# A decoder layer on one core: weights and first operands in one lasting pool, the residual kept by tokens and turned in place, norms inside the gates, loads in program order

## The chip, the cores and the metric

One NeuronCore of a Trainium2 chip runs the whole kernel. Its engines work side by side, each through its own list of instructions in order: TensorE (PE: matmuls and transposes, results in PSUM, 8 banks of 128 x 512 float32), VectorE (DVE), ScalarE (ACT), GpSimd (POOL) and SyncE (SP), which here issues DMAs; POOL issues DMAs too. The metric is the time of one execution on the device in microseconds. An edit is judged by the medians of several runs, and its reasons by the profile of one execution.

## The reference, cut to what matters

```python
h = x                                            # (512 tokens, 1024)
h = h + 0.5 * swiglu(rms_norm(h, g_ffn1), w_ffn1_gu, w_ffn1_down)      # 1024 -> 2 x 2816 -> 1024
h = h + hybrid_mixer(rms_norm(h, g_mix), ...)    # gated conv + stick-breaking attention, 8 heads
h = h + memory_cross_attention(rms_norm(h, g_cross), rms_norm(mem, g_mem), ...)
h = h + 0.5 * swiglu(rms_norm(h, g_ffn2), w_ffn2_gu, w_ffn2_down)
out = rms_norm(h, g_final)

def swiglu(x, w_gu, w_down):
    gate, up = jnp.split(x @ w_gu, 2, axis=-1)
    return (jax.nn.silu(gate) * up) @ w_down
```

All is float32. The kernel multiplies in float32r: each operand is split into a high part `hi` and a low part `lo` (ScalarE makes `hi`, VectorE subtracts to make `lo`), and three matmuls, hi-hi, hi-lo and lo-hi, stand for one product.

## The kernel before, in words

**Four stages in a row:** FFN1, mixer, cross attention, FFN2. Each FFN is `up` (gate and up columns, then the gated values, spilled to DRAM) and `down`. Both use Strassen's scheme in Winograd's form: 7 products in place of 8 on halves of the operands. In `up` the columns come in blocks, five of 512 and one of 256 of each half; a block is 7 products in the order 1, 2, 5, 3, 6, 7, 4 (`UP`), each of two token tiles x 12 matmuls of 128x512, 24 in all. The left operands ("sides", `make_side`, L458) are made once, in the first block, from h times the norm's gain; their sums are on POOL (`sum_`, L465). The right operands are weight tiles of 512 KB: `x1`, `x2`, `x3` are loaded by SP (`load`, L392); sums of weights are made by a DMA on POOL that adds onto a loaded tile (L425) or by VectorE (L423). Each is split into `whi` and `wlo` (L117, L123) four units ahead of its use; loads are asked for five ahead. The first block uses three accumulating DMAs onto `x1` (`DMA_ONLY`).

**Norms.** The root mean square is not put into the operands: it scales rows of the products. `evac_of` multiplies by `r.cols` or its negative when a product leaves PSUM (L489, L492); so the first evacuation needs the norm. In FFN1 the squares are summed by 64 one-column matmuls (`norm1`, L662); in FFN2 by `rf.reduce` (L282) right after the mixer.

**Residual.** `h` is kept by channels: 8 chunks of 128 channels x 512 tokens. `down` makes tokens x channels, so it adds to a second copy `ht`, which FFN1 loads afresh (`in_xr`, 2 MB, POOL, L677) and FFN2 makes by 32 transposes (`turn_back`). After FFN1 32 transposes and 8 copies bring it back into `h` (L692, L693), and only then the mixer's operands `xm` are split (L119, L125).

**Mixer and cross attention** are a list of steps (`prog`), run by `run` (L164): weights come as 1 MB `raw` blocks by SP, halves are split two steps ahead, and each tile of results is 24 matmuls (`tile_step`). The mixer's pool holds 61 tiles of 128x512 for everything that lives.

**Memory and order.** SBUF is given out in phases: a phase's pools (`s` 14 sides, `w` weights, `e`, `a`, `h`; then the mixer's `w`, `a` 61, `c`) are given up at its end, and a tile of the next phase waits until the tiles that lay at its address are released. Tiles of one tag rotate through a fixed number of buffers. The program is written as one list, but a planner orders it: it goes through the instructions by priority, which is the order of writing, with estimated costs, and gives each engine the first instruction that is ready by its estimate. So work that is written later can be issued earlier, DMAs too.

Of the kernel before, what the change touches and what calls it, by code (L numbers as in the profile page):

```python
# [58 lines left out]
def layer_kernel(ctx, tc, xt, xr, memt, consts, g_final, w_gu1, w_dn1, w_dt1, w_qk, w_v, w_cx, w_cb, w_gate,  # L59
# [6 lines left out]
    dram = ctx.enter_context(tc.tile_pool(name="dram", bufs=1, space=bass.MemoryType.DRAM))  # L66
    pools = {}

# [14 lines left out]
    def act_tile(dt=F32, shape=(P, S)):  # L83
        return pools["a"].tile(list(shape), dt, tag="A", name=nm("a"))
# [26 lines left out]

    def mul(out_, a, b):
        nc.vector.tensor_tensor(out=out_, in0=a, in1=b, op=ALU.mult)  # L113
# [14 lines left out]
    def split(src, scale=None):  # L128

        hi = act_tile(F32R)  # L130
        lo = act_tile(F32R)
        split_hi(hi, src, scale)
        split_lo(lo, src, hi, scale)
        return hi, lo
# [29 lines left out]
    def run():  # L164
# [7 lines left out]
        def load():  # L172
            block = blocks[len(raws)]
            raw = pools["w"].tile([P, 2048], F32, tag="raw", name=nm("raw"), bufs=2)
            nc.sync.dma_start(out=raw[:, :block.shape[-1]], in_=block)
            raws.append(raw)

        def prepare(n):
# [4 lines left out]
            m = block.shape[-1] // 2  # L183
            hi = pools["w"].tile([P, 1024], F32R, tag="whi", name=nm("whi"))
            lo = pools["w"].tile([P, 1024], F32R, tag="wlo", name=nm("wlo"))
            src = raws[at][:, half * m:(half + 1) * m]
            split_hi(hi[:, :m], src)
            split_lo(lo[:, :m], src, hi[:, :m])
            parts[n] = tuple(t[:, :m].rearrange("p (k c) -> p k c", c=width) for t in (hi, lo))
# [67 lines left out]
    class Norm:  # L257


        def __init__(self, n=S):  # L260
            self.n, self.acc = n, None

        def square(self, h):
            sq = act_tile()[:, :self.n]
# [82 lines left out]
    class Plan:  # L347


        def __init__(self):  # L350
            self.steps, self.units, self.loads, self.loaded = [], [], [], 0

# [29 lines left out]
    class Weights:  # L382
# [4 lines left out]
        def __init__(self, plan, tiles, n, chain):  # L387

            self.plan, self.src, self.n, self.t, self.at, self.chain = plan, tiles, n, {}, {}, chain
            self.size = [q[0].shape[-1] for q in tiles]  # L390

        def load(self, x, u):  # L392
            def fn():
                tag = x if u < 4 or x == "x2" else x + "b"
                t = pools["w"].tile([P, 1024], F32, tag=tag, name=nm(x), bufs=xbufs[tag])[:, :self.size[u]]
                nc.sync.dma_start(out=t, in_=self.src[u][self.STARTS[x]])
                self.t[x, u] = t

            self.at[x, u] = self.plan.load(fn)
# [13 lines left out]
        def make(self, i, u):  # L413
            x, *then = self.chain[i]
            x = self.t[x, u]
            hi, lo = (pools["w"].tile([P, 1024], F32R, tag=tag, name=nm(tag), bufs=xbufs["w"])
                      for tag in ("whi", "wlo"))
# [6 lines left out]
            elif then[0] is not None:  # L424
                nc.gpsimd.dma_start(out=x, in_=self.src[u][then[0]], accum_op=ALU.add)  # L425
# [10 lines left out]
    xbufs = dict(x1=4, x1b=2, x2=3, x3=4, x3b=2, w=5)  # L436

    def up(g, r, w_gu, begin, norm):

        
        plan, parts = Plan(), {}
        spilled = dram.tile([P, 7, len(PAIRS), 256], F32, name=nm("spilled"))
        negr = spool.tile([P, 4], F32, tag="negr", name=nm("negr"))
# [6 lines left out]
        def prepare():  # L450
            x = [pools["e"].tile([P, 4, S], F32, tag="E", name=nm("x")) for _ in range(2)]
            box["a11"], box["a21"], box["a12"], box["a22"] = (x[k][:, :, s:s + 256] for k in range(2) for s in (0, 256))
            for k in range(KC):
                nc.scalar.activation(x[k // 4][:, k % 4, :], h[k], AF.Copy, scale=col(g, k))
# [780 lines left out]
```

## Time and profile before

| | us |
|---|---|
| median of 3 runs (1433.69 to 1441.03) | 1434.96 |
| the profiled execution | 1434.07 |
| its span, from the first to the last instruction | 1432.1 |
| TensorE busy in the span (97%) | 1384.2 |
| VectorE (66%), ScalarE (52%), POOL (8%) | 949.7, 737.9, 112.0 |
| moved by DMA | 211.37 MB, 148 GB/s on average |

In the profile TensorE's matmuls are pipelined: one starts before the last has ended, so its busy time is nearly the span whatever its pace. The pace is read from the starts of successive matmuls. FFN1's `up` runs from the start to about 252 us, its `down` to 366; the mixer and the cross attention to 1065; FFN2 to the end.

### The profile page before, as it was taken

How to read it: one execution, taken by the hardware profiler on the slowest of the kernel's cores; microseconds unless marked ns; L12 is line 12 of the kernel's file. 1: busy time of each engine (PE TensorE's matmuls, PEld its weight loads, DVE VectorE, ACT ScalarE, POOL GpSimd, SP SyncE). 2: the span in 40 equal slices, each digit the busy share in tenths (PEclk: the TensorE clock that was granted, in tenths of full speed). 3: DMA queues.
4: the chain of work that ended last, by engine and by line, in shares of the span. 5: the costliest groups of instructions: out<-in, count | busy, mean ns of one | idle time of the engine just before them, and what ended most of it. 6: DMA issues, size and time to landing. Idle time of an engine off the chain costs nothing.

```text
span 1432.1 us, 16800 instructions
## 1 busy us (share of the span) xinstructions
PE 1384.2 (97%) x6548; PEld 1160.5 (81%) x6548; DVE 949.7 (66%) x1264; ACT 737.9 (52%) x951; POOL 112.0 (8%) x118
## 2 busy tenths in 40 slices
PE   8999998899899999999999999999979999999997
PEld 7788888688788888888888888988866788878885
DVE  5777777597556663676544446745549787767796
ACT  6655555365455654555533225444436555555563
POOL 4011111110000000000000000000005111011010
PEclk8999999999999999999999999999998999999999
DMA  9877667962422133122232224353329666678571
GB/s 307 193 198 190 181 181 210 271 144 81 170 95 89 60 118 118 59 93 84 88 102 105 88 92 141 122 176 124 112 82 284 163 161 165 182 211 241 180 184 59
DMA packets 50031, 211.37 MB, mean 148 GB/s; under 512 B 5344, under 2 KB 5344, under 8 KB 41120
## 3 DMA queue, kind: packets, MB, share of 16 engines
q1 hardware_dynamic: 33200, 149.22, 30.1%
q0 software_dynamic: 16752, 61.09, 19.4%
q8 instruction: 51, 0.84, 0.2%
q14 instruction: 28, 0.23, 0.0%
HBM read 188.00 MB, written 22.28 MB: 147 GB/s over the span
## 4 chain that ended last, share of the span: by engine, by line
PE 79%; issue 7%; DMA 5%; DVE 5%; ACT 3%; POOL 1%; ACTq 0%; POOLq 0%; DVEq 0%
PE ps L153 13%; PE ps L155 13%; PE ps L154 13%; PE ps L433 10%; PE ps L434 10%; PE ps L432 10%; DMA x<-in_w_gu 3%; DVE wlo L123 2%; DMA x<-in_w_dn 2%; PE ps L250 2%; PE ps L249 2%; PE ps L251 2%; PE z L812 1%; ACT whi L117 1%; PE ps L523 1%
## 5 line engine op out<-in xcount | busy, mean ns | idle before, releaser
L432 PE MATMUL ps<-whi,s 128*128 128x512 f32 (+1 forms) x980 | 379.2, 388 | 17.0 <-ACT whi L117 9.5
L433 PE MATMUL ps<-wlo,s 128*128 128x512 f32 (+1 forms) x980 | 376.8, 385 | 6.4 <-DVE wlo L123 6.4
L434 PE MATMUL ps<-whi,s 128*128 128x512 f32 (+1 forms) x980 | 375.3, 383 | 0.1
L123 DVE TENSOR_TENSOR wlo<-x,whi 128x1024 fp32r<-128x1024 f32 (+1 forms) x238 | 291.6, 1232 | 114.3 <-ACT whi L117 113.1
L117 ACT ACTIVATE whi<-x 128x1024 fp32r<-128x1024 f32 (+1 forms) x238 | 243.8, 1032 | 208.7 <-PE ps L434 135.9
L153 PE MATMUL ps<-a,whi 128*128 128x512 f32 (+1 forms) x832 | 318.2, 383 | 3.8 <-ACT whi L117 3.8
L155 PE MATMUL ps<-a,wlo 128*128 128x512 f32 (+1 forms) x832 | 318.0, 382 | 0.0
L154 PE MATMUL ps<-a,whi 128*128 128x512 f32 (+1 forms) x832 | 317.7, 382 | 0.0
L117 ACT ACTIVATE whi<-raw 128x1024 fp32r<-128x1024 f32 x120 | 127.1, 1060 | 268.7 <-PE ps L154 176.0
L432 PEld LDWEIGHTS ps<-whi,s 128*128 128x128 f32 x980 | 188.7, 193 | 54.4 <-ACT whi L117 10.0
L433 PEld LDWEIGHTS ps<-wlo,s 128*128 128x128 f32 x980 | 188.7, 193 | 43.9 <-DVE wlo L123 10.2
L434 PEld LDWEIGHTS ps<-whi,s 128*128 128x128 f32 x980 | 188.6, 192 | 35.2 <-DVE s L123 0.8
L123 DVE TENSOR_TENSOR wlo<-raw,whi 128x1024 fp32r<-128x1024 f32 x120 | 146.7, 1223 | 84.2 <-ACT whi L117 84.0
L153 PEld LDWEIGHTS ps<-a,whi 128*128 128x128 f32 x832 | 157.1, 189 | 34.0 <-ACT whi L117 4.1
L155 PEld LDWEIGHTS ps<-a,wlo 128*128 128x128 f32 x832 | 157.0, 189 | 31.1 <-DVE wlo L123 0.8
L154 PEld LDWEIGHTS ps<-a,whi 128*128 128x128 f32 x832 | 157.0, 189 | 30.4 <-DVE a L125 0.2
L425 POOL DMA_DIRECT2D x<-in_w_gu x52 | 45.6, 876 | 1037.8 <-DVE wlo L123 1030.6
L423 DVE TENSOR_TENSOR x<-x,x 128x1024 f32<-128x1024 f32 (+1 forms) x60 | 71.0, 1188 | 1.2
L117 ACT ACTIVATE a<-a 128x512 fp32r<-128x512 f32 (+2 forms) x61 | 34.0, 557 | 59.4 <-DVE a L113 19.3
L113 DVE TENSOR_TENSOR a<-ps,a 128x512 f32<-128x512 f32 (+1 forms) x56 | 36.2, 651 | 38.9 <-PE ps L155 38.6
L123 DVE TENSOR_TENSOR a<-a,a 128x512 fp32r<-128x512 f32 (+2 forms) x61 | 36.3, 601 | 15.5 <-ACT a L117 11.6
L489 ACT ACTIVATE a<-ps,ny 128x512 f32<-128x512 f32 (+1 forms) x48 | 31.0, 650 | 29.4 <-PE ps L434 26.9
(163 smaller groups left out, 1312.1 us busy)
## 6 DMA issues: line engine op xcount, KB each, us to landing
x<-in_w_gu SPq DMA_DIRECT2D x66, 512.0 KB, 6.2
x<-in_w_gu POOLq DMA_DIRECT2D x52, 512.0 KB, 6.7
spilled<-e POOLq DMA_DIRECT2D x22, 896.0 KB, 7.6
x<-in_w_dn SPq DMA_DIRECT2D x30, 512.0 KB, 5.5
s<-spilled SPq DMA_DIRECT2D x28, 512.0 KB, 5.2
x<-in_w_dn POOLq DMA_DIRECT2D x20, 512.0 KB, 7.8
raw<-in_w_qk SPq DMA_DIRECT2D x8, 1024.0 KB, 4.9
raw<-in_w_v SPq DMA_DIRECT2D x8, 1024.0 KB, 4.9
```

The lines of the kernel that those rows point to most:

```text
L113: nc.vector.tensor_tensor(out=out_, in0=a, in1=b, op=ALU.mult)
L117: nc.scalar.activation(hi, src, AF.Copy)
L123: nc.vector.tensor_tensor(out=lo, in0=src, in1=hi.bitcast(F32), op=ALU.subtract)
L153: nc.tensor.matmul(ps, wh, xh, start=first, stop=False, **kw)
L154: nc.tensor.matmul(ps, wh, xl, start=False, stop=False, **kw)
L155: nc.tensor.matmul(ps, wl, xh, start=False, stop=last, **kw)
L423: nc.vector.tensor_tensor(out=dst, in0=dst, in1=src, op=ALU.add)
L425: nc.gpsimd.dma_start(out=x, in_=self.src[u][then[0]], accum_op=ALU.add)
L432: nc.tensor.matmul(ps, ah, bh, start=first and k == 0, stop=False, **kw)
L433: nc.tensor.matmul(ps, ah, bl, start=False, stop=False, **kw)
L434: nc.tensor.matmul(ps, al, bh, start=False, stop=last and k == len(parts) - 1, **kw)
L489: nc.scalar.activation(a[key], ps, func, scale=scale)
```

## The change

- **A lasting pool** `kept` is opened once and never given up: 4 weight tiles `x1`, 3 each of `whi` and `wlo`, 2 operand tiles `E`, 8 tiles `A`, 2 tiles `first`. FFN weights, the mixer's weights (now in halves of 512 KB) and the memory's operands come through the same `x1`, `whi`, `wlo`. The phases keep the rest: 12 side tiles (were 14), more weight tiles, and in the mixer 43 tiles (were 61); the 16 tiles of `xm`, and later of `xc`, lie in `A` and `E` (`front`), two pairs in `first`.
- **Tags turn between stages** (`tags`): `down` takes `x1` in the buffers of `x3` and the reverse; the second column block exchanges `x1` and `x2`.
- **Residual by tokens in place:** `h_all` becomes 128 x 8 x 4 x 128 and holds either channels or tokens. `in_xr` is stored in that order and loaded into it at the opening; `ht` is gone. After FFN1 the upper four chunks are turned between products 2 and 4 of `down`, the lower four in steps around the first half accumulations of head 0's q and k (`first_part`, upper chunks first). `turn_back` goes in place, chunk by chunk.
- **Norms in the gates:** products leave PSUM unscaled; `r.cols` scales Silu and the gate product. `norm1` is eight ScalarE squares with an accumulator over `h_all`; in both FFNs it is written behind side 5 in place of side 2.
- **Sides straight from h** with the gain in the split, by chunks; of the four sums one stays on POOL and three are on VectorE.
- **Loads in program order:** `dma` ties each DMA of a queue behind the previous one of that queue. In the first column block loads 4 to 7 go by POOL, and loads are asked for two ahead there. x comes in four quarters, weights between them.

```diff
+    kept = ctx.enter_context(tc.tile_pool(name="kept", bufs=1))
+    KEPT = dict(x1=((P, 1024), 4), whi=((P, 1024), 3), wlo=((P, 1024), 3), E=((P, 4, S), 2), A=((P, S), 8),
+                first=((P, 1024), 2))
+    def dma(out_, in_, queue="sync", **kw):
+        engine = getattr(nc, queue)
+        if queue in last:
+            with tc.issue_after(last[queue].ins):
+                last[queue] = engine.dma_start(out=out_, in_=in_, **kw)
+        else:
+            last[queue] = engine.dma_start(out=out_, in_=in_, **kw)
...
-                        self.start_loads(x.need + 1 + LOADS_AHEAD)
+                        self.start_loads(x.need + 1 + (LOADS_AHEAD if x.need not in (0, 1, 2, 3) else 2))
...
-                tag = x if u < 4 or x == "x2" else x + "b"
-                t = pools["w"].tile([P, 1024], F32, tag=tag, name=nm(x), bufs=xbufs[tag])[:, :self.size[u]]
-                nc.sync.dma_start(out=t, in_=self.src[u][self.STARTS[x]])
+                t = weight_tile(self.tags[x] + ("b" if u >= 4 and x != "x2" else ""))[:, :self.size[u]]
+                dma(t, self.src[u][self.STARTS[x]], "gpsimd" if place in self.plan.behind else "sync")
...
-                nc.gpsimd.dma_start(out=x, in_=self.src[u][then[0]], accum_op=ALU.add)
+                dma(x, self.src[u][then[0]], "gpsimd", accum_op=ALU.add)
...
+        def sums():
+            a11, a21, a12, a22 = (box[k] for k in ("a11", "a21", "a12", "a22"))
+            t, v, w = (half(side_tile(F32)) for _ in range(3))
+            for k in range(4):
+                nc.scalar.activation(t[:, k], a21[:, k], AF.Copy, scale=col(g, k))
+            nc.gpsimd.tensor_tensor(out=box["s3"], in0=a11, in1=a21, op=ALU.subtract)
+            for out_, x, g0, y, op in ((v, a22, 4, t, ALU.subtract), (w, a11, 0, v, ALU.add),
+                                       (box["s4"], a12, 4, w, ALU.subtract)):
+                for k in range(4):
+                    nc.vector.scalar_tensor_tensor(out=out_[:, k], in0=x[:, k], scalar=col(g, g0 + k), in1=y[:, k],
+                                                   op0=ALU.mult, op1=op)
...
+                for k in range(4):
+                    gain = col(g, gains + k)
+                    split_hi(half(hi)[:, k], src[:, k], gain)
+                    split_lo(half(lo)[:, k], src[:, k], half(hi)[:, k], gain)
+            if i == 5:
+                norm()
...
+        dma(cst, consts, "gpsimd")
+        quarter(0, 0)
+        plan.start_loads(2)
+        quarter(1, 0)
+        plan.start_loads(4)
+        quarter(0, 256)
+        quarter(1, 256)
...
+        dma(h_all, xr, "gpsimd")
+        sums = spool.tile([P, 8], F32, tag="sums1", name="sums0", bufs=2)
+        for tok in range(4):
+            for half in range(2):
+                squares_of(tok, half, sums)
+        r1.newton(add_halves(sums))
...
+        down(spilled, residual, w_dn1, w_dt1, lambda: None, squares,
+             {(2, 8): upper, (4, 4): lambda: turn_tokens(range(4), (0, 1))})
...
-    mixer_pools = phase(w=3, a=61, c=1)
+    mixer_pools = phase(a=43, c=1)
...
-    q_step(0)
-    k_step(0)
+    step(lambda: turn_tokens(range(4), (2,)))
+    step(lambda hi, lo: first_part(0, range(4, KC), hi, lo), qk_blocks[0], 0)
+    step(lower)
+    step(lambda hi, lo: first_part(1, range(4, KC), hi, lo), qk_blocks[0], 1)
+    step(lambda: first_part(0, range(4)))
+    step(lambda: first_part(1, range(4)))
```

## Rows read from the trace of the kernel before

**Rows 1.** the page's 40 slices of the span, TensorE's busy tenths

```profile
PE   8999998899899999999999999999979999999997
```

**Rows 2.** windows: PE, PEld, DVE, ACT, POOL busy (count), granted clock, DMA share, GB/s

```profile
0.00:64.30 64.30, 56.27 (x248) 46.35 (x249) 38.60 (x47) 42.09 (x53) 20.09 (x21) 0.89 0.95 276
10.00:20.00 10.00, 9.75 (x46) 7.84 (x46) 5.25 (x4) 9.47 (x14) 7.19 (x4) 0.78 1.05 366
...
278.60:290.90 12.30, 7.09 (x18) 5.04 (x18) 6.52 (x8) 7.01 (x8) 0.00 (x0) 0.72 0.57 185
366.30:379.70 13.40, 9.52 (x46) 7.38 (x45) 10.22 (x24) 12.51 (x23) 1.42 (x4) 0.75 0.55 190
1065.30:1122.40 57.10, 45.51 (x177) 34.92 (x177) 47.07 (x49) 36.82 (x44) 19.96 (x14) 0.88 0.96 273
```

**Rows 3.** timeline, PE at the opening: start, us, what, idle before, releaser

```profile
10.67 1.22 PE L432 MATMUL ps<-whi,s 128*128 128x512 f32 x2
...
63.63 0.39 PE L432 MATMUL ps<-whi,s 128*128 128x512 f32 x1
...
64.31 0.39 PE L432 MATMUL ps<-whi,s 128*128 128x512 f32 x1
```

**Rows 4.** groups by line and shape: count | busy us, mean ns | idle

```profile
L123 DVE TENSOR_TENSOR wlo<-raw,whi 128x1024 fp32r<-128x1024 f32 x120 | 146.7, 1223 | 84.2 <-ACT whi L117 84.0
...
L668 PE MATMUL z<-ones,a 128*128 128x1 f32 x64 | 9.1, 265 | 1.7 <-ACT a L666 1.7
...
L117 ACT ACTIVATE a<-a 128x256 fp32r<-128x256 f32 x16 | 6.6, 410 | 16.4 <-DVE a L789 14.0 <-DVE a L113 2.4
...
L125 DVE SCALAR_TENSOR_TENSOR a<-raw,cst,a 128x256 fp32r<-128x256 f32 x8 | 3.8, 480 | 0.0
```

**Rows 5.** timeline of the turn inside FFN1, POOL and ScalarE

```profile
263.78 0.79 POOL L677 DMA_DIRECT2D ht<-in_xr  x1 [4.75 <-DMA spilled<-e]
...
266.99 0.91 POOL L425 DMA_DIRECT2D x<-in_w_dn  x1 [2.42 <-DVE wlo L123]
...
282.37 1.06 ACT L117 ACTIVATE whi<-x 128x1024 fp32r<-128x1024 f32 x1 [10.63 <-DMA x<-in_w_dn]
```

**Rows 6.** timeline of PE, the same place in FFN2

```profile
1348.97 0.50 PE L433 MATMUL ps<-wlo,s 128*128 128x512 f32 x1 [0.81 <-DVE wlo L123]
```

**Rows 7.** timeline from FFN1 to the mixer: SP, PE, ACT

```profile
366.32 0.33 SPq L175 DMA_DIRECT2D raw<-in_w_qk  x1
...
366.36 3.79 PE L692 MATMUL ps<-ident,ht 128*128 128x128 f32 x32
373.99 0.79 PE L153 MATMUL ps<-a,whi 128*128 128x512 f32 x1 [3.84 <-ACT whi L117]
...
368.40 3.99 ACT L693 ACTIVATE h<-ps 128x512 f32<-128x512 f32 x8
```

**Rows 8.** timeline from the mixer to FFN2: SP, PE, DVE, POOL

```profile
1065.27 19.11 SPq L396 DMA_DIRECT2D x<-in_w_gu  x13
...
1073.71 1.22 PE L432 MATMUL ps<-whi,s 128*128 128x512 f32 x2 [5.01 <-ACT whi L117]
...
1092.66 0.57 PE L433 MATMUL ps<-wlo,s 128*128 128x512 f32 x1 [2.68 <-DVE wlo L123]
...
1077.10 10.27 DVE L123 TENSOR_TENSOR wlo<-x,whi 128x1024 fp32r<-128x1024 f32 x3
...
1079.67 3.27 POOL L465 TENSOR_TENSOR x<-x 128x1024 f32<-128x1024 f32 x1
```

**Rows 9.** timeline of SP, FFN1's down weights in the opening

```profile
26.82 0.46 SPq L396 DMA_DIRECT2D x<-in_w_dn  x1
```

**Rows 10.** DMA issues: queue, count, KB each, median us to landing

```profile
x<-in_w_gu POOLq DMA_DIRECT2D x52, 512.0 KB, 6.7
...
ht<-in_xr POOLq DMA_DIRECT2D x1, 2048.0 KB, 14.8
out_t<-ht SPq DMA_DIRECT2D x8, 256.0 KB, 2.2
```

More of the change, by code (lines that the diff above doesn't have):

```diff
@@ L182, in prepare @@
                 load()
[L183 to L189, printed above, removed]
+            hi, lo = kept_tile("whi", F32R), kept_tile("wlo", F32R)
+            src = raws[at][half]
+            split_hi(hi, src)
+            split_lo(lo, src, hi)
+            parts[n] = tuple(t.rearrange("p (k c) -> p k c", c=width) for t in (hi, lo))
         ready = used = 0
@@ L351, in __init__ @@
             self.steps, self.units, self.loads, self.loaded = [], [], [], 0
+            self.behind = ()
         def step(self, fn):
@@ L415, in make @@
             x = self.t[x, u]
-            hi, lo = (pools["w"].tile([P, 1024], F32R, tag=tag, name=nm(tag), bufs=xbufs["w"])
-                      for tag in ("whi", "wlo"))
+            parity["n"] += 1
+            hi, lo = (weight_tile(tag + ("" if parity["n"] % 5 < 3 else "b"), F32R) for tag in ("whi", "wlo"))
             m = self.size[u]
@@ new lines, in squares_of, with add_halves @@
+    def squares_of(tok, half, sums):
+        sq = side_tile(F32)[:, :S]
+        nc.scalar.activation(sq.rearrange("p (k c) -> p k c", c=P), residual(tok, half), AF.Square,
+                             accum_out=sums[:, 4 * half + tok:4 * half + tok + 1])
+    def add_halves(sums, n=4):
+        both = spool.tile([P, n], F32, tag="both", name=nm("both"))
+        nc.vector.tensor_tensor(out=both, in0=sums[:, :n], in1=sums[:, 4:4 + n], op=ALU.add)
+        return both
+    def norm1():
+        dma(h_all, xr, "gpsimd")
+        sums = spool.tile([P, 8], F32, tag="sums1", name="sums0", bufs=2)
+        for tok in range(4):
+            for half in range(2):
+                squares_of(tok, half, sums)
+        r1.newton(add_halves(sums))
@@ new lines, in layer_kernel, with turn_tokens, split_turned, squares @@
+    turned = {}
+    def turn_tokens(ms, ts):
+        for m in ms:
+            if m not in turned:
+                turned[m] = bank()
+        for t in ts:
+            for m in ms:
+                nc.tensor.transpose(out=turned[m][:, t * P:(t + 1) * P], in_=h_all[:, m, t, :], identity=ident)
+    def split_turned(ms):
+        for m in ms:
+            ps = turned.pop(m)
+            xm[m] = split(ps, col(G_MIX, m), room[(m + 4) % KC])
+            nc.scalar.activation(h[m], ps, AF.Copy)
+    with phase(s=12, w=1):
+        spilled = up(G_FFN1, r1, w_gu1, load_x, None, norm1)
+        sums = spool.tile([P, 8], F32, tag="sums1", name="sums1", bufs=2)
+        def squares(i, t):
+            part = {2: (t, 0), 3: (t, 1), 7: (t + 2, 1), 4: (t + 2, 0)}.get(i)
+            if part is not None:
+                squares_of(*part, sums)
+        def upper():
+            room.extend(front())
+            for m in range(4, KC):
+                turn_tokens([m], range(4))
+                split_turned([m])
+        down(spilled, residual, w_dn1, w_dt1, lambda: None, squares,
+             {(2, 8): upper, (4, 4): lambda: turn_tokens(range(4), (0, 1))})
+        rm.newton(add_halves(sums))
```

327 lines of the change are left out of this document (158 added, 169 removed).

## The prediction, made before the change was run

> **What bounds the kernel now.** I read the page's slices first [rows 1]: TensorE is full (a 9) in most slices, and the slices below that stand together, at the opening, at slices 7 and 8, at slice 11, at slice 30 and at the end. So TensorE bounds the kernel, and only the stretches in which it is interrupted can give time back. A busy TensorE is not one at its peak, so I then went by matmul starts: three steps take 0.68 us at the end of the first gate/up column block [rows 3], 0.227 us for a 128x512 matmul. A column block of gate/up is 7 products of 24 matmuls, 168, which is 38.1 us of work.
>
> The windows view [rows 2] then gives the losses. *Opening:* the first column block is done at 64.31 [rows 3] and holds 38.1 us of work; 26.2 us are lost. *Turn inside FFN1:* 278.6 to 290.9 holds 18 matmuls, 4.1 us of work in 12.3; 8.2 lost. *FFN1 to mixer:* 366.3 to 379.7 holds 32 transposes (3.8 us, [rows 7]) and 14 matmuls (3.2); 6.4 lost, of which 3.84 is idle [rows 7] and 2.6 the low clock after it. *Mixer to FFN2:* 1065.3 to 1122.4 is again one column block; 57.1 less 38.1 is 19.0 lost. In all 59.8 us. The granted clock's mean is 0.72 to 0.89 in these windows, so the lower level has a part in each.
>
> What each waits for is in the timeline. In the turn, the 2 MB load of `ht` goes out on POOL at 263.78, the accumulating weight load behind it at 266.99, and ScalarE's next `whi` starts at 282.37 after 10.63 us of idling [rows 5]. From FFN1 to the mixer, the transposes start at 366.36, eight copies occupy ScalarE from 368.40 for 3.99 us, and TensorE goes on at 373.99, released by a `whi` of a weight whose load was issued at 366.32 [rows 7]. From mixer to FFN2, 13 weight loads start together at 1065.27, when the mixer's pool is given up; TensorE goes on at 1073.71; then three `wlo` splits take 10.27 us of VectorE while POOL adds operands, and TensorE waits another 2.68 at 1092.66 [rows 8].
>
> **Opening.** The 64 one-column norm matmuls leave TensorE (9.1 us busy, [rows 4]); they become eight Square activations over a token-major copy of x. Side 1 becomes four gain splits of 128x256: 4 x 0.41 on ScalarE and 4 x 0.48 on VectorE [rows 4], where a whole scaled copy of x stood before. I put the first matmul at about 8.5 instead of 10.67 [rows 3]. The counterweight is bytes: `xr`, 2 MB, is now loaded here as well, on POOL, and `ht` no longer is later. I count what the first block's last product must have: 4 transfers of 512 KB for x, 4 for xr, 6 direct and 8 accumulating weight loads, and the first 5 of the next block, which are queued in between; 27 x 0.524 is 14.2 MB. At the 276 GB/s of the opening [rows 2] that is 51.3 us; the last split (1.06 and 1.22, [rows 4, 5]) and half a product (2.7) end the block at 56.3. Before, four loads of down weights (1.6 MB; the first is [rows 9]) were pulled ahead into the opening; in program order they are not. Gain 64.3 - 56.3 = 8.0. Bounds: with no byte waited for, 8.5 + 38.1 + 2.6 at the low clock = 49.2, a gain of 15.1; if the 2 MB stand wholly ahead of the next accumulation (7.6 us at 276 GB/s) and only the 2.2 us of the earlier start are won, -5.
>
> The norm's root is no longer a factor of the first evacuations but of Silu and of the gate product, so nothing of it holds a PSUM bank before the seventh product; its cover is five products of 5.4 us. The evacuations change operation, not length; I cost them at nothing.
>
> **Turn inside FFN1.** With the 2 MB gone, the accumulation has POOL's queue to itself. The same place in FFN2, which has no such load, idles only 0.81 before the matmul at 1348.97 [rows 6]. I take the difference of 7.4, and a little less for two side tiles fewer (12 for 14): 7.0 of 8.2. Bounds 4 and 8.2. The side loads are now one product later, with some 15 us before they are used.
>
> **FFN1 to mixer.** The upper half's 16 transposes, splits and copies go between the last two products of down, where TensorE has their banks and the evacuations are over; the lower half's run beside half accumulations of head 0 (2 x 12 matmuls, 5.4 us). After the last down matmul come an evacuation, four transposes (0.5, an eighth of [rows 7]), ScalarE's half of a split (0.5, as one of the eight copies) and VectorE's; VectorE needs 0.48 for half the size [rows 4], so under 1 each: at most 3 us, below that cover. The transposes themselves stay (3.8). The first mixer weights go into buffers that the finished `x3` chain frees, so their load no longer starts at the end. Gain 6 of 6.4; bounds 3 and 6.4. If the cover fails, the price is that 3 and the low clock again.
>
> **Mixer to FFN2.** The first four weight loads use the lasting `x1` buffers, and the first side the lasting `first` pair, with operands (the lower half of the residual) that are final four tiles of 24 matmuls, 22 us, before the mixer ends. Nothing of product 1 then waits for the mixer's pool, and the planner does pull ready work forward [rows 9]. I take it that product 1 follows the last mixer matmul at 1065.3. What is late next is product 5's weight, third in line: its accumulation is queued on POOL behind a load that may need the freed pool; three issues of 0.9 [rows 5], 6.7 to land [rows 10] and 2.3 to split give 1077.2, against 1076.2 for TensorE after two products. VectorE gets three of POOL's four sums as twelve 128x256 operations (12 x 0.48 = 5.8 us, [rows 4]), but is spared the 6.6 us by which three `wlo` went over 3 x 1.22 [rows 4, 8]. I leave 5 us of the 19.0 in place and take 14. Bounds: 18 if only one wait is left; 7 if only the shorter operand chain counts: an evacuation (1), four splits and one `whi` (4 x 0.41 + 1.06) after 1065.3 start product 1 at 1069.0, 4.7 earlier, and the 2.68 of waiting on POOL's sums goes.
>
> **Mixer and tail.** The mixer's pool keeps 43 tiles and 18 more in the lasting pool for the same 61; its weights come in halves of 512 KB at a low DMA share. No row shows what a shortage would cost, since TensorE has none there now. The output goes out in pieces of 512 B: nearest row 2.2 us for 256 KB [rows 10]. I charge 1.5 for both; bounds 0 and 6.
>
> **Sum.** 8.0 + 7.0 + 6.0 + 14.0 - 1.5 = 33.5. The profiled execution took 1434.07 (span 1432.1 and 2.0 around), 0.9 below the median of the runs; 1434.1 - 33.5 = **1400.6**.
>
> **A rule weighed.** POOL's row says 14.8 us for the 2 MB of xr while other loads ran [rows 10]. The Trainium skill, "DMA: Bandwidth & Descriptors", section "Anatomy of one DMA — SWDGE (gpsimd) path", gives a fixed 2.0 us and 436 GB/s beyond it for a DMA from that queue, an estimate of 6.8 us. The trace does not agree under load. By that rule the opening would not be byte-bound: the rival just below.
>
> **Rivals.** *The opening is not bound by bytes.* From 10 to 20 us the DMA engines moved 366 GB/s [rows 2]; at that rate 14.2 MB need 38.8 us and TensorE's own 49.2 decides. Total 1434.1 - (15.1 + 7 + 6 + 14 - 1.5) = 1393.5. For it: loads in need order. Against: 276 over the whole opening, with accumulations in it. Chance 0.12.
>
> *FFN2's start is not pulled forward*, so that the change there doesn't do what it is built for: the x3 loads, first on POOL, wait for the pool, everything behind them too, and splits stay behind the last residual add. Gain 7 instead of 14: 1407.6. For it: in one program order an early wait holds all later ones. Chance 0.17.
>
> *The opening loses*: xr stands ahead of the accumulations, and eight squares on ScalarE wait for it with every `whi` behind them. -5 instead of 8: 1413.6. For it: 14.8 us for the same load [rows 10]. Chance 0.14.
>
> *Slower: the pinned SP queue.* Loads can no longer pass one that waits for a buffer. If at each column block's start the third pair sits behind a second pair whose buffer is late, each of the eight boundaries between full blocks could wait half a landing (3.4, [rows 10]) and run 2.6 at the low clock, an estimate of 48 us: 1448.6. It decides from 33.5 / 8 = 4.2 us a boundary. Against: in full stretches loads already go out in that order, a few us ahead of their use. Chance 0.06. *The mixer runs short of tiles*: two gate evacuations wait and hold banks; if splits pile up behind them I price it at 20 us, 1420.6. Chance 0.06.
>
> **How the numbers follow.** The forecast has 0.45. All largest gains together (15.1 + 8.2 + 6.4 + 18) end at 1386, the smallest (-5 + 4 + 3 + 7 - 6) at 1431; together they are unlikely, and 1386 to 1424 leaves out the slow rival, the worst of the tile shortage and little else. About 0.5%, 7 us, is what a measurement of this kernel can tell from no change. Faster by more: all of the first four cases but a twentieth, and half of the tile shortage, 0.87. Within: 0.06. Slower: 0.07.
>
> **What would show it.** Right: no 128x1 matmul in the opening and the first block over before 58; no wait of several us near the last down accumulation of FFN1; mixer matmuls within 1 us of the last down matmul; product 1 of FFN2 directly behind the mixer, with its loads some 10 us earlier. Wrong: ScalarE idle on xr in the opening, SP's loads late at block boundaries, TensorE idle inside the mixer.

## The result, and the profile after it

The changed kernel took 1417.3 us (median; 1414.97 to 1421.65) where the kernel before, run beside it, took 1436.45: a ratio of 0.9867, 95% interval 0.9831 to 0.9903. The same code run again beside other kernels took 1412.9 (1411.77 to 1414.44), ratio 0.9829 (0.9811 to 0.9848). So the change gains 19 to 25 us where 33.5 were forecast; the time lies in the forecast range, 12 to 17 us above its point. The two medians of one code stand 4.4 us apart: totals nearer than that tell nothing here, and what follows goes by stretches of the profiles, between the starts of two matmuls. A block's end is the start of the matmul behind its 168th; the changed kernel already runs five of the next block among these. The kernel before has one profile, so that its own scatter is not in the gains below. One run of e3 (1716.9, granted clock 0.75 where the others had 0.98 to 0.99) is left out below.

| stretch (us) | before | after | after, again | gain | forecast |
|---|---|---|---|---|---|
| start to end of FFN1's block 0 | 64.31 | 61.56 | 61.87 | 2.4 to 2.8 | 8.0 |
| from there to the end of FFN1 | 301.82 | 301.32 | 300.92 | 0.5 to 0.9, with 24 transposes more (2.8): 3.3 to 3.7 | 7.0 |
| to the last matmul of the mixer | 698.95 | 689.32 | 689.36 | 9.6, of which those 2.8: 6.8 | 6.0 |
| to the end of FFN2's block 0 | 57.32 | 48.45 | 47.09 | 8.9 to 10.2 | 14.0 |
| to the last matmul of FFN2, and the tail | 309.71 | 312.62 | 310.82 | -2.9 to -1.1 | -1.5 |

(The 2.8 is 24/32 of the 3.79 in [rows 7].) Three terms of five came out at 0.3 to 0.7 of their size. The page and its windows, in the columns of [rows 1, 2]:

```profile
PE   7999998899999999999999999999999999999997
```

```profile
0.00:61.56 61.56, 48.82 (x184) 38.08 (x185) 43.85 (x70) 40.59 (x69) 15.74 (x24) 0.94 0.90 270
...
274.00:290.00 16.00, 13.27 (x52) 10.23 (x51) 12.78 (x15) 9.98 (x12) 0.00 (x0) 0.89 0.83 285
363.00:377.00 14.00, 14.00 (x68) 11.56 (x67) 10.63 (x32) 7.44 (x12) 0.00 (x0) 1.00 0.39 133
1052.20:1100.65 48.45, 43.59 (x179) 34.56 (x177) 38.22 (x65) 31.21 (x46) 7.94 (x10) 0.93 0.73 185
```

The dips of slices 11 and 30 are gone, and the mixer's start is full at full clock (363 to 377: busy 14.00 of 14.00, clock 1.00). The opening's slices and the turn still lose. The timeline of the opening, all engines, shows where:

```profile
8.84 1.22 PE L458 MATMUL ps<-whi,first 128*128 128x512 f32 x2 [4.00 <-ACT whi L144]
...
18.51 5.40 DVE L504 SCALAR_TENSOR_TENSOR s<-E,cst,s 128x256 f32<-128x256 f32 x8 [0.85 <-DMA E<-in_xt]
23.84 1.66 DVE L504 SCALAR_TENSOR_TENSOR E<-E,cst,s 128x256 f32<-128x256 f32 x4
...
12.57 0.91 POOL L135 DMA_DIRECT2D h<-in_xr  x1
19.42 2.63 POOL L500 TENSOR_TENSOR E<-E 128x1024 f32<-128x1024 f32 x1 [5.93 <-DVE s L504]
28.32 0.91 POOL L135 DMA_DIRECT2D x<-in_w_gu  x1 [6.26 <-DVE wlo L150]
...
27.83 0.80 PE L459 MATMUL ps<-wlo,s 128*128 128x512 f32 x1 [2.83 <-DVE wlo L150]
...
30.87 0.64 ACT L714 ACTIVATE s<-h 128x512 f32<-128x512 f32 x1 [4.76 <-DMA h<-in_xr]
...
36.74 0.57 ACT L534 ACTIVATE A<-ps 128x512 f32<-128x512 f32 x1
...
37.36 0.58 PE L458 MATMUL ps<-whi,s 128*128 128x512 f32 x1 [2.87 <-ACT A L534]
```

Product 1 starts at 8.84, as forecast (8.5). Then two queues are late. VectorE's operand sums wait for x's last quarter (18.51) and take 5.40 for eight beside POOL's one; product 5's `wlo` comes behind them, and the first accumulation behind a product 5 weight goes out only at 28.32. And ScalarE idles 4.76 until `xr` has landed, 18.3 us after its issue at 12.57; the eight squares follow, then a split of product 3's side, and behind that, at 36.74, the copy that frees product 3's bank. The low clock stood from 27.4 to 30.8 and again from 37.6 to 41.1, each time from about the end of one of these stalls of TensorE. After 37.36 TensorE waits for nothing more in this opening.

The turn, in the same view:

```profile
243.18 0.47 SPq L135 DMA_DIRECT2D x3b<-in_w_dn  x1
243.69 0.52 SPq L135 DMA_DIRECT2D x3b<-in_w_dt  x1
...
267.10 0.90 POOL L135 DMA_DIRECT2D x3b<-in_w_dn  x1 [9.11 <-DVE wlo L150]
...
276.06 1.06 ACT L144 ACTIVATE whib<-x3b 128x1024 fp32r<-128x1024 f32 x1 [5.27 <-DMA x3b<-in_w_dn]
...
279.34 0.50 PE L458 MATMUL ps<-whib,s 128*128 128x512 f32 x1 [2.24 <-ACT s L144]
```

ScalarE's wait on an accumulation has shrunk from 10.63 [rows 5] to 5.27, but TensorE's next wait, 2.24, is on a side load. Those loads need the last write of `spilled`. The view of DMA issues, cut to 255 to 258 us, has that write in the changed kernel (queue, count, size, us to landing), and cut to 255 to 259 us the same write in the kernel before:

```profile
spilled<-E POOLq DMA_DIRECT2D x1, 896.0 KB, 9.0
```

```profile
spilled<-e POOLq DMA_DIRECT2D x1, 896.0 KB, 5.1
```

And from the mixer to FFN2:

```profile
1022.16 37.23 SPq L135 DMA_DIRECT2D x<-in_w_gu  x8
...
1055.42 1.87 PE L308 MATMUL z<-ones,A 128*128 128x1 f32 x8 [2.83 <-DVE A L299]
1057.15 0.77 PE L458 MATMUL ps<-whi,first 128*128 128x512 f32 x1
```

The weights load from 1022 on, 30 us before the mixer's last matmul; in [rows 8] they start with its end. But product 1 starts 4.95 us behind the mixer's last matmul (1052.20): the norm's eight one-column matmuls stand ahead of it in TensorE's order and wait for VectorE's sum of squares.

### The profile page after: what moved, and what is told of

It is laid out like the page before. It is cut to its first block, busy times and chain, and to the rows that moved or that the text cites. A ratio compares the mean times of both kernels' runs of the same rounds, so it can differ in the third digit from the quotient of the medians.

```text
span 1413.3 us, 16964 instructions
## 1 busy us (share of the span) xinstructions
PE 1369.7 (97%) x6484; PEld 1147.5 (81%) x6484; DVE 951.7 (67%) x1312; ACT 733.6 (52%) x983; POOL 101.2 (7%) x121
## 4 chain that ended last, share of the span: by engine, by line
PE 80%; DMA 8%; issue 5%; DVE 4%; ACT 2%; POOL 0%; SPq 0%; ACTq 0%; POOLq 0%; DVEq 0%
PE ps L179 13%; PE ps L181 13%; PE ps L180 13%; PE ps L458 10%; PE ps L459 10%; PE ps L460 10%; DMA x3b<-in_w_dn 4%; DMA x<-in_w_gu 2%; PE ps L276 2%; PE ps L275 2%; PE ps L277 2%; DMA h<-in_xr 1%; PE z L882 1%; DVE wlo L150 1%; ACT whi L144 1%
## 5 line engine op out<-in xcount | busy, mean ns | idle before, releaser
L144 ACT ACTIVATE whi<-x 128x1024 fp32r<-128x1024 f32 x249 | 262.0, 1056 | 364.8 <-PE ps L180 136.9
L150 DVE TENSOR_TENSOR wlo<-x,whi 128x1024 fp32r<-128x1024 f32 x249 | 305.0, 1229 | 144.0 <-ACT whi L144 140.0
L458 PE MATMUL ps<-whi,s 128*128 128x512 f32 (+1 forms) x532 | 202.9, 382 | 6.3 <-ACT A L534 3.3
L459 PE MATMUL ps<-wlo,s 128*128 128x512 f32 (+1 forms) x532 | 201.5, 379 | 2.8 <-DVE wlo L150 2.8
L460 PE MATMUL ps<-whi,s 128*128 128x512 f32 (+1 forms) x532 | 201.6, 379 | 0.3 <-DVE s L150 0.3
L458 PE MATMUL ps<-whib,s 128*128 128x512 f32 (+1 forms) x352 | 137.2, 390 | 8.6 <-ACT A L534 4.0
L460 PE MATMUL ps<-whib,s 128*128 128x512 f32 (+1 forms) x352 | 135.6, 385 | 0.5 <-DVE s L150 0.5
L458 PEld LDWEIGHTS ps<-whi,s 128*128 128x128 f32 x532 | 100.4, 189 | 26.6 <-ACT A L534 4.5
L460 PEld LDWEIGHTS ps<-whi,s 128*128 128x128 f32 x532 | 100.8, 189 | 19.8 <-DVE s L150 0.7
L179 PE MATMUL ps<-a,whi 128*128 128x512 f32 (+1 forms) x304 | 111.7, 367 | 0.0
L181 PE MATMUL ps<-a,wlo 128*128 128x512 f32 (+1 forms) x304 | 111.5, 367 | 0.0
L180 PE MATMUL ps<-a,whi 128*128 128x512 f32 (+1 forms) x304 | 111.5, 367 | 0.0
L179 PE MATMUL ps<-A,whi 128*128 128x512 f32 x256 | 99.8, 390 | 0.0
L179 PE MATMUL ps<-E,whi 128*128 128x512 f32 x256 | 99.7, 390 | 0.0
L180 PE MATMUL ps<-E,whi 128*128 128x512 f32 x256 | 99.7, 389 | 0.0
L180 PE MATMUL ps<-A,whi 128*128 128x512 f32 x256 | 99.6, 389 | 0.0
```

The source lines that it names most:

```text
L144: nc.scalar.activation(hi, src, AF.Copy)
L150: nc.vector.tensor_tensor(out=lo, in0=src, in1=hi.bitcast(F32), op=ALU.subtract)
L179: nc.tensor.matmul(ps, wh, xh, start=first, stop=False, **kw)
L180: nc.tensor.matmul(ps, wh, xl, start=False, stop=False, **kw)
L181: nc.tensor.matmul(ps, wl, xh, start=False, stop=last, **kw)
L458: nc.tensor.matmul(ps, ah, bh, start=first and k == 0, stop=False, **kw)
```

## The experiments

All are edits of the changed kernel. Stretches in us: A, start to the end of FFN1's block 0; B, from there to the end of FFN1; C, from the mixer's last matmul to product 1 of FFN2; D, from the mixer's last matmul to the end of FFN2's block 0. The mixer took 689.3 to 689.4 in every one.

| kernel | median (range) | A | B | C | D |
|---|---|---|---|---|---|
| changed | 1417.3 (1415.0 to 1421.7) | 61.6 | 301.3 | 4.95 | 48.5 |
| e1 norm later | 1419.6 (1416.9 to 1423.2) | 66.4 | 302.4 | 0.23 | 47.2 |
| e2 no squares | 1415.4 (1414.3 to 1419.8) | 64.9 | 300.4 | 4.13 | 47.2 |
| e4 tail loads free | 1420.9 (1419.2 to 1422.8) | 65.6 | 302.0 | 4.13 | 47.3 |
| e5 unpinned | 1417.0 (1413.5 to 1422.2) | 65.8 | 299.2 | 4.13 | 46.7 |
| a2 changed, again | 1412.9 (1411.8 to 1414.4) | 61.9 | 300.9 | 4.13 | 47.1 |
| e3 sum late | 1420.1 (1419.7 to 1426.2) | 64.6 | 302.6 | 4.33 | 49.0 |
| e6 no accumulate | 1409.4 (1408.7 to 1413.5) | 58.7 | 300.8 | 4.13 | 44.0 |
| e7 xr later | 1422.1 (1421.4 to 1424.0) | 61.3 | 308.1 | 4.94 | 48.8 |
| e8 vector sums | 1422.0 (1419.1 to 1426.1) | 59.9 | 303.3 | 4.75 | 52.7 |
| e9 loads wait | 1413.0 (1411.3 to 1416.6) | 63.2 | 303.5 | 4.77 | 48.2 |
| e10 own buffers | 1417.8 (1416.0 to 1421.7) | 61.4 | 305.2 | 3.48 | 48.6 |
| e11 together | 1422.3 (1419.0 to 1425.1) | 65.5 | 308.9 | 0.23 | 48.3 |

Where the code of a stretch is the same, A lay at 61.6, 61.9 and 63.2 (e9), B at 300.4 (e2), 300.9, 301.3 and 303.5 (e9), D at 47.1, 47.2 (e2), 48.5 and 48.8 (e7): one profile doesn't tell less than 2 to 3 us apart. What comes after D took 310.7 to 313.7 in all but e4 (317.0) and e6 (314.3).

**e1, the norm later.**

```diff
-            if i == 5:
+            if i == 5 and load_rows is not None:
+                load_rows()
+            if i == 6:
                 norm()
...
                 elif i == 3:
                     copy(("u", t), ps, -1.0)
+                    if first:
+                        silu(t)
```

> The changed kernel with its two FFN norms made later: the root of the norm is asked for with side 6 instead of side 5, and in the first column block Silu stands with product 3 instead of product 2; xr's load keeps its place. Theory: at the start of FFN2 the four one-column matmuls of the norm stand ahead of product 1 in TensorE's order, and cost its 2.83 us of idling at 1052.2 and some 2 us at the low clock after it; behind products 1 and 2 they cost nothing, so block 0 of FFN2 ends about 4 us earlier against the start of the mixer. In the opening the squares stand behind two more splits and one evacuation, so of the 2.87 us before product 3 about 2 go. Together 5 to 7 us faster than the changed kernel, some 1410 to 1412. Rival: what holds product 1 there is its operands (weights, sides), not the norm; then TensorE idles as long under another name, and the total changes by less than 2 us.

```profile
1058.36 0.39 PE L458 MATMUL ps<-whi,first 128*128 128x512 f32 x1
...
1077.10 1.06 ACT L144 ACTIVATE whib<-x 128x1024 fp32r<-128x1024 f32 x1 [2.58 <-DMA x<-in_w_gu]
1079.92 1.06 ACT L144 ACTIVATE whib<-x 128x1024 fp32r<-128x1024 f32 x1 [1.76 <-DMA x<-in_w_gu]
1080.88 0.58 ACT L536 ACTIVATE A<-ps 128x512 f32<-128x512 f32 x1
...
1081.52 0.66 PE L458 MATMUL ps<-whi,s 128*128 128x512 f32 x1 [2.43 <-ACT A L536]
```

In the timeline product 1 now follows the mixer within 0.23, yet the block ends where it did (D 47.2). TensorE waits 20 us later instead: for a copy that frees its bank and that stands on ScalarE behind two `whib`, each waiting for an accumulating load. The norm took its place ahead of product 1, but moving it alone gave no time back. (This edit also moves Silu in the first block; e11 below moves the norm and not Silu, with the same end.) In the opening the moved norm and Silu made A 3 to 5 longer; the 2 us forecast there didn't come.

**e2, no squares.**

```diff
-        for tok in range(4):
-            for half in range(2):
-                squares_of(tok, half, sums)
+        nc.vector.memset(sums, 512.0)
```

> The changed kernel without the eight Square sums of the first FFN (their sums are set to a constant; its output is not the reference's); xr is still loaded at the same place. Theory: the squares, which wait on ScalarE for xr's landing at 30.84 and then take 5 us, hold the evacuation of product 5 and with it product 3; without them the 2.87 us of idling before product 3 and the low clock behind it (1.7 us) go: block 0 ends at about 57 instead of 61.56, the total falls by 4 to 5 us. Rival: the opening is bound by bytes, as forecast; then block 0 ends within 1 us of 61.56, since the accumulations land when they did, and idling moves to product 6 or 4.

The idle time before product 3 is gone, but A is no shorter. In this run x's last quarter landed at 23.9 instead of 18.4, which made product 5's stalls 5.07 and 3.13; that hides what the squares cost. Later, at 52.35, TensorE waits 2.80 for VectorE, whose queue stands behind splits of accumulated weights. e3 and e7 show the squares better.

**e3, POOL's sum late.**

```diff
-            nc.gpsimd.tensor_tensor(out=box["s3"], in0=a11, in1=a21, op=ALU.subtract)
...
+            if i == 7:
+                with tc.issue_after(last["gpsimd"].ins):
+                    nc.gpsimd.tensor_tensor(out=box["s3"], in0=box["a11"], in1=box["a21"], op=ALU.subtract)
```

> The changed kernel, but the one operand sum left on POOL (s3, for product 7) is issued behind the accumulations of product 4's weights instead of beside VectorE's eight sums. Theory: in the opening those eight took 5.40 us at 18.51 while POOL's sum ran from 19.42 to 22.05; alone they take 4.1 (1.67 for four in the start of FFN2, 3.3 for eight), so product 5's wlo and side come 1.5 to 2 us earlier, its stall of 2.83 us shrinks to about 1, the accumulations behind its splits go out at 26.5 for 28.3, and block 0 ends 1 to 2 us earlier. Total 1 to 3 us faster than the changed kernel. Rival: the sums wait for x's last quarter and the sharing costs nothing; then the eight still take over 5 us and nothing moves.

```profile
19.48 3.26 DVE L503 SCALAR_TENSOR_TENSOR s<-E,cst,s 128x256 f32<-128x256 f32 x8 [2.43 <-DMA E<-in_xt]
...
26.73 0.80 PE L459 MATMUL ps<-wlo,s 128*128 128x512 f32 x1 [1.66 <-DVE wlo L150]
...
27.22 0.89 POOL L135 DMA_DIRECT2D x<-in_w_gu  x1 [13.85 <-DVE wlo L150]
...
37.47 0.79 PE L458 MATMUL ps<-whi,s 128*128 128x512 f32 x1 [4.09 <-ACT A L536]
```

The steps came as expected, but not the gain. Alone, the eight sums take 3.26 instead of 5.40. The Trainium skill, "SBUF — State Buffer", section "Who interferes with whom", says that a VectorE instruction with two SBUF inputs contends with a GpSimd one that reads SBUF. The trace agrees: in the changed kernel one of the eight takes 2.62 beside POOL's sum of 2.63, the others under 0.5 each. The stall shrinks from 2.83 to 1.66 and the accumulations leave 1.1 earlier. But product 3 starts at 37.47, as in the changed kernel (37.36): the squares, held by `xr`, decide it, and what came earlier is idled away (4.09 for 2.87). A, 64.6, is even 1.4 to 3.1 longer, with 6.8 us of low clock around the end of that wait instead of 3.4 and further waits at 55 (1.29) and 59 us (0.56); the total is no better.

**e7, xr later.**

```diff
     def norm1():
-        dma(h_all, xr, "gpsimd")
...
         spilled = up(G_FFN1, r1, w_gu1, load_x, None, norm1)
+        dma(h_all, xr, "gpsimd")
```

> The changed kernel with xr's 2 MB load moved from the opening to just ahead of the down projection's loads, and without the eight Square sums that read it (set to a constant; its output is not the reference's). Against e2, which left the squares out alone, it prices the 2 MB in the opening. Theory (bytes): the four SP loads behind xr land 4 to 6 us earlier, product 5's accumulations too, and block 0 ends at 55 to 57, 5 to 9 us ahead of e2's 64.94 and 5 ahead of the changed kernel. But at the turn the 2 MB stand again where they were before the change, and cost 2 to 5 us there. Total between 4 us faster and the same. Rival: the 2 MB ride along on idle engines; then block 0 ends where e2's does, within 1.5 us, apart from x's last quarter.

The DMA view from 28 to 44 us in 40 slices (busy tenths of the DMA engines, and GB/s):

```profile
DMA  0000000893988999889999999999999999999999
GB/s 0 0 0 0 0 0 0 102 123 41 123 164 164 195 225 256 154 174 236 195 205 215 277 379 410 410 389 338 297 256 215 225 225 205 205 195 246 195 215 215
```

Neither squares nor the 2 MB are in this opening, and it is no shorter (61.3). It ends 3.6 before e2's, where x's last quarter landed 3.7 later (23.9 for 20.2 here). So the rival holds there: the bytes don't bind. From 28 to 30.8 the DMA engines stand idle, while POOL waits for VectorE's `wlo` to send the first accumulation (29.51), and then accumulations follow one another; ScalarE's splits wait for their landings up to 51.2. The price is in B, 7.7 longer than in e2, which differs by that load alone, and 4.6 longer than the longest B of the same code. It falls ahead of the turn, though, in FFN1's last gate/up block, since the load goes out there (POOL, then TensorE):

```profile
226.00 0.88 POOL L135 DMA_DIRECT2D h<-in_xr  x1
...
241.07 0.58 PE L458 MATMUL ps<-whib,s 128*128 128x256 f32 x1 [4.23 <-ACT A L534]
```

**e6, no accumulations in the first blocks.**

```diff
-            elif then[0] is not None:
+            elif then[0] is not None and self.chain is not Weights.DMA_ONLY:
```

> The changed kernel without the eight accumulating weight loads of the first column block of each FFN (its products take the weights unsummed; its output is not the reference's). Theory: both starts are bound by the chain load, split, accumulate, split on POOL's queue, whose landings follow one another by 2.5 us (37.80 to 50.28 in the opening, 1074 to 1084 in FFN2). Without it block 0 of the first FFN ends at 57 to 59 (the waits for xr's squares and product 5's operands stay), block 0 of FFN2 2 to 3 us earlier against its start. Total 5 to 7 us faster. Rival: the accumulations land in time, and what is left at both starts are ScalarE's and VectorE's queues; then both blocks end within 1 us of where they did.

About as expected in both starts: A 58.7, D 3.1 to 4.4 shorter, total 1409.4. This kernel leaves the additions out, so it is no faster version, only a bound on what their chain costs. It is the only edit that shortened both; with the chain gone xr's load also goes out at 3.5 us, so that A's gain isn't the chain's alone. Product 1 of FFN2 still starts 4.13 behind the mixer.

**e4 and e5, the order of loads.** In e4 four loads of each FFN leave the program order, in e5 all:

```diff
-                dma(t, self.src[u][self.STARTS[x]], "gpsimd" if place in self.plan.behind else "sync")
+                if u >= 4 and x != "x2":
+                    nc.sync.dma_start(out=t, in_=self.src[u][self.STARTS[x]])
+                else:
+                    dma(t, self.src[u][self.STARTS[x]], "gpsimd" if place in self.plan.behind else "sync")
```

```diff
-        if queue in last:
-            with tc.issue_after(last[queue].ins):
-                last[queue] = engine.dma_start(out=out_, in_=in_, **kw)
...
+        engine.dma_start(out=out_, in_=in_, **kw)
```

> The changed kernel, but the four loads of each FFN's last down weights (x1b and x3b) are not held to the program order of their queue, so that they may go out as early as their buffers allow, as in the kernel before. Theory: issued at 243 to 267 they crowd the stretch before the turn, and the accumulation on x3b, issued at 267.10, and the side load landing at 278.42 come late for that; with the tail loads gone from there TensorE's 2.24 us of idling at 276.7 and the low clock after it shrink by at least 2.5 us, and the same place in FFN2 loses nothing. In the opening the 1.5 MB cost 0 to 2 us, if they go out there. Total 1 to 3 us faster. Rival: the side loads wait for their pool of 12 tiles and for the spilled write, not for the channel; then the idling at 276.7 stays within 0.5 us and the total is the same or up to 2 us slower.

> The changed kernel with every load left to the planner's order of its queue, as in the kernel before; all else is kept. If the program order of loads is a part of the gain (weights in the order of need), undoing it costs 3 to 10 us, in the opening above all. If holding loads in order is what makes them crowd together ahead of the turn and costs the 2 us losses at 224, 233, 276 and in FFN2, this one is 3 to 8 us faster than the changed kernel. My theory gives it little either way: within 4 us, a gain at the turn (tail weights early) against a loss in the opening.

e4's theory fell: the tail loads went out at 19.6 to 21.0 in the opening, and at the turn TensorE waits longer than in the changed kernel (3.99 at 283.31, for 2.24) on the same side load. The same place in FFN2, which was to lose nothing, loses too: TensorE waits 2.45 at 1328.33 and runs 6.8 us at the low clock, and that is where the 317.0 after D comes from. In the opening the loads do harm. From 28 to 44 us the DMA view of e4 has

```profile
x<-in_w_gu POOLq DMA_DIRECT2D x8, 512.0 KB, 12.0
```

against 8.7 us in the changed kernel, and A is 2.3 to 4.0 longer: what is in flight together with the accumulations costs, what lands as they begin (xr) doesn't. e5 has the same loss in the opening and wins at the turn: its last `spilled` write lands in 4.7 us, and the first 120 matmuls of `down` take 27.3 where they take 33.0 to 35.4 in the profiles with program order and the same code there. Most of that is lost again just ahead of them and behind them: B, 299.2, is the shortest, but only 1.2 below the least of the same code. So the program order of loads is worth 2.5 to 4 us in the opening and costs something at the turn, less than one profile can size; the total is the same.

**e9, FFN2's loads wait.**

```diff
-                        dict(x1="x2" if b == 1 else "x1", x2="x2" if b > 1 else "x1", x3="x3"))
+                        dict(x1="x3", x2="x2", x3="x3") if b == 0 and source is not None else
+                        dict(x1="x1" if source is not None else "x2" if b == 1 else "x1", x2="x2" if b > 1 else "x1", x3="x3"))
```

> The changed kernel with the part undone that lets FFN2's first weights load while the mixer runs: the first column block's weights of FFN2 use buffers of the FFN's own pool, which the mixer's tiles cover until its end, as before the change. Theory: the early loads are what product 1 of FFN2 gained; without them it starts as far behind the mixer as before the change, 8 to 10 us behind the last mixer matmul instead of 5, and block 0 of FFN2 ends 4 to 8 us later; the total is 4 to 8 us slower than the changed kernel, 1418 to 1423. Rival: the gain comes from the shorter operand chain and VectorE's free queue, not from the loads; then block 0 of FFN2 ends within 2 us of the changed kernel's and the total stays at 1413 to 1417.

Half an undoing: product 1's two loads still went out at 1020.9, presumably since the tiles over their buffers were given up early. The next two waited until 1055.8, which is 14 and 17 us later against the last mixer matmul than in the changed kernel, and product 5's two accumulations went out 15 and 11 later. That cost nothing that shows (D 48.2, C 4.77, both within the scatter of the same code). The early loads of product 1 weren't tried.

**e8, e10 and e11, towards a faster version.** e8 lets VectorE make half of the sums that accumulations make; e10 adds

```diff
-                        Weights.EARLY if b else Weights.DMA_ONLY,
-                        dict(x1="x2" if b == 1 else "x1", x2="x2" if b > 1 else "x1", x3="x3"))
+                        Weights.EARLY,
+                        dict(x1="x1", x2="x2", x3="x3"))
```

(e8 has the first of the two lines), and e11 three edits more: FFN2's norm with side 3, POOL's sum with side 6, and loads free of the order from FFN1's third block to its end.

> The changed kernel, but in the first column block of each FFN the weight sums of products 5 and 6 are made by VectorE (as in the other blocks) instead of by accumulating loads: 4 accumulations in the block instead of 8, 4 additions of 128x1024 more (1.22 us each). Theory: the chain of accumulations, which alone is worth 2.8 to 3.6 us in each start (e6), is half as long; block 0 of the first FFN ends at 59.5 to 61, block 0 of FFN2 41.5 to 42.5 after its first product (43.5 and 42.95 in the changed kernel). Total 2 to 5 us faster than the changed kernel, 1408 to 1412. Rival: VectorE is the tighter queue from 18 to 37 us, and the additions delay the splits behind them; then both blocks end 1 to 3 us later and the total is slower.

> As e8 (VectorE makes the sums of products 5 and 6 in the first column block of each FFN too), but the first two blocks' weights use the buffers that the later blocks use (first operands the four x1, second the three x2). Theory: e8's loss in FFN2 is block 1's first weights, which in it wait for an x2 buffer that the longer chain holds until product 4 (no SP load between 1038.78 and 1080; TensorE idle 4.19 at 1087.23 on that weight). With buffers of their own they load early again: block 0 of the first FFN ends at 58.5 to 60.5 and block 1 39.9 later (41.1 in e8), block 0 of FFN2 ends 41.5 to 43 after its first product (47.9 in e8). Total 2 to 4 us faster than the changed kernel, 1409 to 1412. Rival: VectorE is too full for the additions at FFN2's start; then block 0 of FFN2 still takes over 45 and the total is no better than the changed kernel's 1413 to 1417.

> e10 with three more edits that the runs point to: the norm of FFN2 asked for with side 3 (product 1 of FFN2 directly behind the mixer, e1), POOL's operand sum issued behind product 3's accumulations (product 5's splits 1.1 us earlier, e3), and loads free of the program order from the third column block of the first FFN to its end (the turn 1.2 us shorter, e5, without that run's loss in the opening). Theory: the gains add where each stretch has one limit: opening 2 to 3, turn 1 to 2, FFN2's start 2 to 4; total 1405 to 1410, 5 to 9 us faster than the changed kernel. Rival: as in e1, e3 and e8, what one stretch gives the next takes back, since the queues of ScalarE and VectorE are full of work that only changes places; then it ends within 3 us of the changed kernel, 1411 to 1417.

e8's opening is as expected (59.9), its start of FFN2 as its rival has it, 4 to 5 us longer. The cause that I named for it, late loads for want of a buffer, is at most a part: in e10 they load early, D is 4.1 shorter than in e8 and no shorter than in the changed kernel, and TensorE still waits 4.74 at that place (4.19 in e8).

```profile
1091.88 0.69 PE L458 MATMUL ps<-whib,first 128*128 128x512 f32 x1 [4.74 <-ACT whib L144]
...
1082.25 1.06 ACT L144 ACTIVATE whi<-x 128x1024 fp32r<-128x1024 f32 x1 [1.95 <-DMA x<-in_w_gu]
1083.33 1.28 ACT L550 ACT_TABLE_LOAD   x1
1084.63 1.34 ACT L550 ACTIVATE A<-A,ny 128x512 f32<-128x512 f32 x2
...
1089.84 1.99 ACT L144 ACTIVATE whib<-x 128x1024 fp32r<-128x1024 f32 x2
```

It is ScalarE: behind a `whi` that waits for an accumulation, a table load, two Silu, a copy, splits of the next side and weights come one after the other, and the split that TensorE needs is the last of them. e10 loses elsewhere too: FFN1's second block takes 43.7 in place of 39.9. e11 joined what looked like gains and lost most: C is 0.23, D is 48.3 all the same, A 65.5 (x's last quarter landed at 21.5), and B 308.9, with 44.4 in FFN1's second block and 34.4 in its last, for 26.5 to 28.3 where loads keep program order and nothing else changed there. No version beat the changed kernel.

## Why the prediction was right and wrong

*Bound and direction: right.* TensorE bounds the kernel, the gain came from the named stretches, and the slower rivals didn't happen: at the full block boundaries SP's pinned loads cost next to nothing (39.9 a block before and after, but for FFN2's second, 41.6 and 40.4), and the mixer shows no shortage of tiles. That the total lies within the range, with three terms at 0.3 to 0.7 of their size, is owed to the range's width.

*Opening, 8.0 forecast, 2.4 to 2.8 measured.* The step that failed is the count of bytes: 14.2 MB at 276 GB/s "that is 51.3 us", with the block's end 5 us behind it. The last accumulation did land at 50.3, but that was luck. With 2 MB fewer it landed no earlier (a split waited for it until 51.2) and the block ended at the same time, with the DMA engines idle for 2.8 us in its midst (e7). And the end came 11 us behind that landing, set by waits of TensorE that were over at 37.36 (in the second profile 1.3 us of waits come later). The rival "not bound by bytes" was right in its condition and wrong in its price of 15.1, since it let TensorE's own work decide. What sets the end are two chains of about the same length: x's last quarter, VectorE's sums, product 5's splits, then accumulations one behind the other; and xr, eight squares, the copy that frees a bank. 1.1 us taken out of the first alone were idled away before product 3 (e3); with the second taken out (e2, e7) TensorE waited later, behind splits of accumulated weights. In e2 and e7 x's last quarter was also late, so what each chain is worth is not shown apart. The rival "the opening loses" had the second chain right and its price wrong.

*Turn, 7.0 forecast, 3.3 to 3.7 measured* (1.1 to 4.2 with the B of e2 and e9). The step that failed is "the accumulation has POOL's queue to itself" with the twin in FFN2 as its measure: the change also lines the loads up in program order, which crowds them ahead of the turn. The last write lands in 9.0 instead of 5.1, and the side loads behind it are late next. Letting the loads go free takes that wait away and makes others (e5, B 299.2, a gain of 5.5 with the transposes); the rest, 1.5 us, stays open. What the removed load cost at its old place no run shows: e7 puts it 38 us earlier, where it costs 4.6 to 7.7.

*FFN1 to mixer, 6.0 forecast, 6.8 measured.* Right, by the steps named: the first mixer matmul starts 0.6 behind the last down matmul (362.88, 363.47). This is read from the trace; no run takes the steps away again. The 0.4 above the bound of 6.4 stays open.

*Mixer to FFN2, 14.0 forecast, 8.9 to 10.2 measured.* "Product 1 follows the last mixer matmul" failed by 4.1 to 4.95: the norm's matmuls, which the forecast left out, stand ahead of it. Taken away alone, that wait gives nothing: made to follow at once (e1, e11), the block ends at the same time, since ScalarE's splits behind accumulations are the next to be late. The accumulations alone are worth 3 to 4.4 (e6), and with them gone the wait ahead of product 1 is 4.13 of the 5.9 us that D still has over its 38.1 of work. So the mis-sized part is the "5 us of the 19.0" left in place; it is 9 to 10.3, held by two chains that end at about the same time. No run takes both away. The early loads, which the forecast thought the heart of it, were not shown to matter (e9). What gave the gain is so not shown apart: product 1's early loads and the shorter operand chain both remain in e9.

*Elsewhere, -1.5 forecast, -2.9 to -1.1 measured.* Near in size by luck: the forecast charged the mixer and the tail, but the mixer shows no loss and the tail 0.2. About half of it (1.7 and 0.5) is FFN2's second column block, the rest mostly FFN2's turn from gate/up to `down`. No run looked for its cause.

## What to carry to other kernels

Where several in-order queues feed one engine, an earlier start was worth nothing until the chain that ends last was shorter: follow each queue (sums, splits, accumulations, copies that free a bank) to the end of the block, and sum the gain from the longest, not from the first wait that goes. That the DMA engines look full doesn't show that bytes bind: they are seven to nine tenths busy from 28 to 44 us of the changed kernel, and 2 MB fewer left the end where it was. Only taking bytes out shows it. A large load that is moved must be counted with what is in flight beside it at the new place.

## What the hardware showed that I had not expected

- With accumulating loads alone in flight the DMA engines are nine tenths busy at 195 to 246 GB/s (the end of e7's rows above), while 10 to 20 us of the kernel before moved 366 GB/s [rows 2]. In the changed kernel's opening the last four of 512 KB landed 2.5 us apart, which is 210 GB/s, and the two plain loads of that size between the accumulations in POOL's queue 1.2 to 1.3 behind what went before: an accumulation took the time of nearly twice its bytes.
- Eight 128x256 sums on VectorE took 5.40 us beside a 2.63 us sum on POOL and 3.26 alone (e3).
- Between profiles with the same code, the last 512 KB quarter of x, issued at 4.4 to 4.7, landed at 18.4 and 18.9 in two, at 22.5 in e9 and at 23.9 in e2, while the first accumulation beside it landed at 18.2 to 18.5 in all four. No run shows why.
